# More Strassen pairs in the gate and up projections of a decoder layer, with the residual stored in DRAM meanwhile and some lo parts formed by a DMA

## Chip, cores and metric

The kernel runs on one core of a Trainium2 chip. The metric is the device time of one execution in microseconds; the median of three runs of the kernel before is 1488.6 us (1488.46 to 1488.66). All data are float32 and 256 tokens are processed.

## The reference

One decoder layer on 256 tokens of width 2048: a mixer (state space heads beside gated short convolutions), a cross-attention to 256 memory tokens, and a SwiGLU feed-forward network of width 5632, each behind an RMSNorm and added to the residual, with a last RMSNorm. What the change touches is the feed-forward network:

```
def swiglu(h, w_gate, w_up, w_down):
    return (jax.nn.silu(h @ w_gate) * (h @ w_up)) @ w_down

h = h + swiglu(rmsnorm(h, norm_ffn[i]), w_gate[i], w_up[i], w_down[i])
```

## The kernel before

**Products in three passes.** TensorE multiplies float32 rounded to a shorter form (fp32r). Each operand is therefore kept as a sum hi + lo of two such numbers, and a product is hi*hi + lo*hi + hi*lo, three matmuls.

**The weight stream.** All weights lie in DRAM in the order of use, as chunks of 128 partitions x 1024 numbers (512 KB): two blocks of 128 rows of a weight matrix by 512 columns. `load_to` (L197) issues their loads on SyncE's queue (SP), each into one of six raw buffers, as soon as one is free. `split_to` makes hi and lo of a chunk: ScalarE copies the raw chunk into h with rounding (L236), VectorE subtracts, l = raw - h (L237). There are four h and four l buffers, so a chunk's copy waits until TensorE has read the h of the chunk four back.

**Plain chunks.** `tok_mm` multiplies one chunk with the two blocks of 128 tokens: first eight matmuls with h (L310, L311), then four with l (L314), twelve in all.

**Blocks of the feed-forward network.** Gate (g) and up (u) are made in 11 blocks (n = 0 to 10) of 512 columns. For each, eight chunks of g and eight of u (c = 0 to 7) are summed in four PSUM accumulators, (g, u) x (two token blocks). `ffn_units` gives the order of the chunks, also that of the weight stream; a unit is one chunk, two, or a pair.

**Strassen pairs.** In blocks 1 to 8 (`SEVEN`) the chunks c = 0 and 1 of g and u are taken as pairs: chunk c of g with chunk c of u, a 2 x 2 product of blocks, in seven products in place of eight (Winograd's form). With three passes that is 21 matmuls for the pair (`seven_mm`, L982 to L985), where two plain chunks have 24. A pair needs sums of weight blocks: `pair_sums` makes four half-chunk sums on VectorE (L211 to L214) and hi and lo of three of them (copies on ScalarE, L218; subtractions on VectorE, L219), six slots of 128 x 512. It needs sums of token blocks, made once by `token_sums` and kept. And four of the seven products go to four shared PSUM accumulators, from which `p_post` forms corrections (one copy on ScalarE, L936; four operations on VectorE, L937 to L940) once the block's last pair is done. `whole` adds a correction to each of the four accumulators of g and u when they are evacuated (L1207).

**After a block.** `g_post` and `u_post` form silu(g) * u (L1216, L1224), turn it by 32 x 32 transposes on VectorE (L329), write it to DRAM (`put`, L342) and read it back transposed (`get`, L349), both on SP, and keep hi and lo of it (L1234, L1235) in four slots for the down projection.

**Slots.** One pool of 63 slots of 128 x 512 holds, in the feed-forward network: the residual (`res`, 8), the normed input (`h2g`, 16), the gated products (4 a block, in the end 44), and the parts of pairs (6 each). The residual is next used when the down projection's pairs and sums are added to it (`p_post`, `d_evac`).

**Order of work.** TensorE and SP run in the order of the code. On ScalarE, VectorE and GpSimd a planner of the framework orders the instructions at build time, by its estimate of when each is ready, with those earlier in the code going first. Work behind a block is written as generators: `step`, called once in each unit after its first part, moves each one to its next `yield`. `ahead_of(i, f)` calls f just ahead of the load of chunk i on SP's queue.

Of the kernel before, what the change touches and what calls it, by code (L numbers as in the profile page):

```python
# [17 lines left out]
F32 = mybir.dt.float32  # L18
F32R = mybir.dt.float32r
AF = mybir.ActivationFunctionType  # L20
ALU = mybir.AluOpType
# [3 lines left out]
T = 256  # L25
# [2 lines left out]
FF = 5632  # L28
FT = FF // 128
FN = FF // 512  # L30
SEVEN = range(1, 9)
OUT_GAPS = (2, 5, 4, 5)
GAPS = (2, 4, 5, 4, 5, 4)
H = 32
# [38 lines left out]
def ffn_units():  # L73


    o = [[((m, 0, c),)] for h in range(2) for m in "gu" for c in range(4 * h, 4 * h + 4)]
    for n in range(1, FN):
        if n in SEVEN:
            for q, rest in ((0, "g2 g3 g4 u2 u3 u4"), (1, "g5 g6 g7 u5 u6 u7")):
                o.append([(("g", n, q), ("u", n, q))])  # L80
                k = [(a[0], n, int(a[1])) for a in rest.split()]
                o += [[(a,), (b,)] for a, b in zip(k[0::2], k[1::2])]
        else:
            o += [[((m, n, c),), ((m, n, c + 1),)] for m in "gu" for c in range(0, KT // 2, 2)]
    return o
# [34 lines left out]
def stream_plan():  # L120

    p = [(("a0",), 512), (("b0",), 512)]
    p += [(("ab", kt), 1024) for kt in range(1, KT)]
    for n in range(2, 22):
        p += [(("in", n, c), 1024) for c in range(KT // 2)]
    p += [(("wo", n, c), 1024) for n, c in out_order()]
    p += [(k, 1024) for k in order_of(out_units())]
    p += [((m, c), 1024) for m in "kqv" for c in range(KT // 2)]
    p += [(("o", n, c), 1024) for n in range(4) for c in range(2)]
    p += [(k, 1024) for k in order_of(ffn_units() + down_units())]  # L130
    return p


def trunk(tc, wst, vecs, xp, xtp, mp, mtp, wdt_in, nfin, outp):
    nc = tc.nc
    plan = stream_plan()
    index = {k: i for i, (k, _) in enumerate(plan)}
    offs, o = [], 0
# [5 lines left out]
    with ExitStack() as ctx:  # L144
# [12 lines left out]
        drp = E(tc.tile_pool(name="scr", bufs=1, space=DRAM))  # L157
# [5 lines left out]
        def nm(s):  # L163
            cnt[0] += 1
            return f"{s}{cnt[0]}"

        def slot(shape=(128, 512), dt=F32):
            return sp.tile(list(shape), dt, tag="s", name=nm("s"))
# [11 lines left out]
        act = nc.scalar.activation  # L180
        tt = nc.vector.tensor_tensor
# [23 lines left out]
        def pair_sums(key, u):  # L205


            g = held.pop(key)
            a, b = slice(0, 512), slice(512, 1024)
            f = bp.tile([128, 1024], F32, tag="b", name=nm("b"))  # L210
            tt(f[:, a], g[:, a], u[:, a], ALU.add)  # L211
            tt(u[:, a], u[:, a], u[:, b], ALU.add)  # L212
            tt(f[:, b], f[:, a], u[:, b], ALU.add)
            tt(g[:, a], f[:, b], g[:, b], ALU.add)  # L214
            pair_parts[key] = []
            for x in (f[:, a], f[:, b], g[:, a]):
                h, l = slot(dt=F32R), slot(dt=F32R)
                nc.scalar.copy(h, x)  # L218
                tt(l, x, h.bitcast(F32), ALU.subtract)  # L219
                pair_parts[key].append((h, l))  # L220

        def split_to(n):
            while nsplit[0] < min(n, len(plan)):
                i = nsplit[0]
                key, w = plan[i]
                r = raws.pop(i)
                if key in first_of:
                    held[key] = r
                elif key in second_of:
                    pair_sums(second_of[key], r)  # L230
                h = hip.tile([128, 1024], F32R, tag="h", name=nm("h"))
                l = lop.tile([128, 1024], F32R, tag="l", name=nm("l"))
                m = 2 if i in (0, 2) else 1
                for j in range(m):
                    c = slice(j * w // m, (j + 1) * w // m)
                    nc.scalar.copy(h[:, c], r[:, c])  # L236
                    tt(l[:, c], r[:, c], h[:, c].bitcast(F32), ALU.subtract)  # L237
                los[i] = l
                his[i] = h
                nsplit[0] += 1  # L240
# [28 lines left out]
        def small(name):  # L269
            return cp.tile([128, 2], F32, tag=name, name=nm(name), bufs=4)  # L270
# [84 lines left out]
        procs = []  # L355
# [68 lines left out]
        def ahead_of(i, f):  # L424
            before.setdefault(i, []).append(f)
# [437 lines left out]
        res = [[None] * 4 for _ in range(2)]  # L863
# [27 lines left out]
        def wait(k):  # L891
            for _ in range(k):
                yield
# [24 lines left out]
        def token_scale(name, sums, factor=None):  # L918

            e = small("rv")  # L920
            with tc.high_priority():
                nc.vector.tensor_reduce(e, sums, axis=mybir.AxisListType.X, op=ALU.add)
            r = inv_rms(e, D)
            out = cp.tile([128, 2], F32, name=name)
            ts(out, r, 1.0 if factor is None else factor, None, ALU.mult)
            return out


        shared, seven_a = {}, {}
# [19 lines left out]
            return  # L949
            yield  # L950

        def token_sums(key, parts):


            xy = fp.tile([128, 1024], F32, tag="f", name=nm("f"))
            w = 512 // len(parts)
            for i, (hi, lo) in enumerate(parts):
                tt(xy[:, i * w:i * w + w], hi.bitcast(F32), lo.bitcast(F32), ALU.add)
            a11, a21, a12, a22, *o = [xy[:, i * 128:i * 128 + 128] for i in range(8)]
            tt(o[0], a21, a22, ALU.subtract)  # L960
            tt(o[1], a11, o[0], ALU.subtract)
            tt(o[2], a21, a11, ALU.subtract)
            tt(o[3], a12, o[1], ALU.subtract)
            seven_a[key] = []
            for i in range(2):
                h, l = [tp.tile([128, T], F32R, tag="t", name=nm("t")) for _ in range(2)]
                y = xy[:, 512 + i * T:512 + i * T + T]
                nc.scalar.copy(h, y)
                tt(l, y, h.bitcast(F32), ALU.subtract)
                seven_a[key] += [(h[:, j * 128:j * 128 + 128], l[:, j * 128:j * 128 + 128]) for j in range(2)]  # L970
# [71 lines left out]
        for i, parts in enumerate(units_o):  # L1042
            for j in (i, i + 1, i + 2):
                if j < len(units_o) and len(units_o[j][0]) == 2 and units_o[j][0][0] not in seven_a:
                    c = units_o[j][0][0][2]
# [6 lines left out]
            _, n, c = keys[0]  # L1052
# [90 lines left out]
        h2g = {}  # L1143
        h2s = cp.tile([128, 2, 4], F32, name="h2s")
        ff = {}

        def o_post(n, accs):
            add_to_res(n, accs, h2s)
            if n == 3:
                ff["r"] = token_scale("fscale", h2s)  # L1150
            if n == 0:
                yield
            yield from to_features(n, "nffn", h2g, None if n == 0 else (4, 1, 0) if n == 1 else (6, 2, 1))
# [23 lines left out]
        with tc.high_priority():  # L1177
            for mb in range(2):
                Vs.append(slot())
                c = scales["mem"][:, mb:mb + 1]  # L1180
# [21 lines left out]
        def whole(m, n, tb, ps):  # L1202

            if n not in SEVEN:
                return ps
# [34 lines left out]
        def part_mm(part):  # L1240
            m, n, c = part[0]
            if len(part) == 2:
                g, u, p = faccs["g", n], faccs["u", n], shared[n]
                seven_mm(part, side_blocks(h2g, 2 * c), seven_a[c], g, u, p,
                         p + [g[0], g[1], u[0]] if c == 0 else [], p if c == 1 else [])
                return
            start = c == 0
            if n in SEVEN:
                start = (1,) if (m, c) == ("u", 2) else False
            tok_mm(faccs[m, n], part[0], side_blocks(h2g, 2 * c), (0, 1), start, c == KT // 2 - 1)  # L1250

        for i, parts in enumerate(ffn_units()):
            if i == len(ffn_units()) - 3:
                token_sums(("d", 0, 0), [gs[0]])
            if i == 8:
                for c in range(2):
                    token_sums(c, [(h2g[2 * c + k][:, 0:T], h2g[2 * c + k][:, T:]) for k in range(2)])
            post = []
            for part in parts:
                m, n, c = part[0]  # L1260
                for k in part:
                    if k[2] == 0:
                        faccs[k[:2]] = [acc(), acc()]
                if len(part) == 2:
                    if c == 0:
                        shared[n] = [msc() for _ in range(4)]
                    else:
                        post.append(p_post(n, shared[n]))
                elif c == KT // 2 - 1:
                    post.append((g_post if m == "g" else u_post)(n, faccs[m, n]))  # L1270
            unit([(list(part), lambda part=part: part_mm(part)) for part in parts], post or None)
# [123 lines left out]
        for i, parts in enumerate(units):  # L1395
# [7 lines left out]
            if len(parts[0]) == 2:  # L1403
                _, n, c = keys[0]
# [4 lines left out]
            n = keys[-1][1]  # L1409
# [136 lines left out]
```

## Time and profile before

| | |
|---|---|
| Median of three runs | 1488.6 us (1488.46 to 1488.66) |
| Profiled execution | span 1487.0 us, first to last instruction; the runs' median is 1.6 us above it |
| TensorE clock granted | 0.998 |
| TensorE matmul, VectorE, ScalarE busy | 99%, 77%, 56% of the span |
| GpSimd busy | 2% |
| DMA | 346.71 MB, mean 233 GB/s |

In the pages and tables that follow, PE is TensorE's matmuls, PEld its weight loads, DVE VectorE, ACT ScalarE, POOL GpSimd, SP SyncE. A row of a group gives line, engine, operation, what it writes and reads, the count, busy time and mean duration, and then how long the engine was idle just before and for whom it waited. A row in order of time gives start and duration in us. Line numbers are those of the kernel before.

Of the span, block 1 of the feed-forward network begins at 822.7 us, block 9 at 1160.0, block 10 at 1203.5, and the down projection at 1247.0.

### The profile page before, as it was taken

What the parts mean: (1) busy time and instruction counts of PE and PEld (TensorE: products, weight loads), DVE (VectorE), ACT (ScalarE), POOL (GpSimd) and SP (SyncE); (2) the same over time, 40 slices, a digit from 0 to 9 for tenths busy, and PEclk for the clock granted to TensorE, in tenths of its full rate; (3) what the DMA queues carried; (4) which work ended last, traced back from release to release, by engine and by line L of the source; (5) the groups of instructions that cost most, each with busy time, mean ns of one, the idle gap of its engine ahead of it and who ended that gap; (6) DMA issues with size and microseconds to landing.
All of it is one profiled execution on the core that took longest, in us unless ns stands there. A gap on an engine that the chain in (4) does not pass through costs nothing.

```text
span 1487.0 us, 18685 instructions
## 1 busy us (share of the span) xinstructions
PE 1476.3 (99%) x6637; PEld 1216.9 (82%) x6637; DVE 1138.9 (77%) x1596; ACT 837.1 (56%) x1176; POOL 33.8 (2%) x46
## 2 busy tenths in 40 slices
PE   9999999999999999999999999999999999999997
PEld 7788888888888888888888888888888888888886
DVE  6677777776785775997577888888887667979975
ACT  7576654867654554665465555555554444655553
POOL 0001000101000000000000000000000000000000
PEclk9999999999999999999999999999999999999999
DMA  9886766868767675768747676665667665765553
GB/s 361 275 282 227 268 225 219 289 225 308 235 214 278 212 233 198 267 228 283 265 159 237 234 248 212 231 213 206 232 226 245 223 225 198 240 215 196 201 189 108
DMA packets 149214, 346.71 MB, mean 233 GB/s; under 512 B 11360, under 2 KB 62976, under 8 KB 149120
## 3 DMA queue, kind: packets, MB, share of 16 engines
q1 hardware_dynamic: 140064, 338.64, 65.6%
q10 hardware_dynamic: 9056, 6.87, 1.5%
q8 instruction: 52, 0.85, 0.2%
q14 instruction: 42, 0.34, 0.1%
HBM read 321.30 MB, written 24.17 MB: 232 GB/s over the span
## 4 chain that ended last, share of the span: by engine, by line
PE 98%; DMA 0%; issue 0%; SPq 0%; ACT 0%; DVE 0%; DVEq 0%; POOLq 0%; POOL 0%
PE a L310 28%; PE a L311 28%; PE a L314 28%; PE m L985 2%; PE m L983 2%; PE m L982 2%; PE a L982 1%; PE a L985 1%; PE a L983 1%; PE m L731 1%; PE m L314 0%; PE m L310 0%; PE m L311 0%; DMA r<-in_w_dram 0%; PE m L1139 0%
## 5 line engine op out<-in xcount | busy, mean ns | idle before, releaser
L237 DVE TENSOR_TENSOR l<-r,h 128x1024 fp32r<-128x1024 f32 (+1 forms) x539 | 650.7, 1215 | 231.3 <-ACT h L236 220.3
L236 ACT CAST h<-r 128x1024 fp32r<-128x1024 f32 (+1 forms) x539 | 562.2, 1047 | 468.4 <-PE a L311 310.2
L310 PE MATMUL a<-h,s 128*128 128x512 f32 x1855 | 726.3, 392 | 0.4 <-ACT h L236 0.4
L311 PE MATMUL a<-h,s 128*128 128x512 f32 x1855 | 722.5, 389 | 0.0
L314 PE MATMUL a<-l,s 128*128 128x512 f32 x1855 | 498.9, 389 | 0.0
L310 PEld LDWEIGHTS a<-h,s 128*128 128x128 f32 x1855 | 348.5, 188 | 74.7 <-issue 2.0
L314 PEld LDWEIGHTS a<-l,s 128*128 128x128 f32 x1855 | 348.4, 188 | 72.5
L311 PEld LDWEIGHTS a<-h,s 128*128 128x128 f32 x1855 | 348.6, 188 | 71.5
L218 ACT CAST s<-b 128x512 fp32r<-128x512 f32 x64 | 38.7, 616 | 23.5 <-DVE b L211 19.8
L329 DVE STREAM_TRANSPOSE b<-s 128x512 f32<-128x512 f32 x62 | 40.7, 689 | 6.4 <-ACT s L336 6.4
L219 DVE TENSOR_TENSOR s<-b,s 128x512 fp32r<-128x512 f32 x64 | 43.2, 683 | 0.0
L672 DVE SCALAR_TENSOR_TENSOR t<-t,vec,t 128x255 f32<-128x255 f32 (+2 forms) x72 | 33.1, 490 | 3.9 <-ACT t L669 3.2
L211 DVE TENSOR_TENSOR b<-r,r 128x512 f32<-128x512 f32 x32 | 21.9, 685 | 14.3 <-DMA r<-in_w_dram 14.2
L336 ACT ACTIVATE s<-a,xr 128x512 f32<-128x512 f32 x42 | 26.4, 679 | 3.6 <-PE a L314 3.6
L1207 DVE TENSOR_TENSOR f<-a,f 128x512 f32<-128x512 f32 x32 | 20.5, 683 | 8.5 <-PE a L314 8.4
L985 PE MATMUL m<-s,t 128*128 128x512 f32 x64 | 24.9, 389 | 0.0
L982 PE MATMUL m<-s,t 128*128 128x512 f32 x64 | 24.9, 389 | 0.0
L983 PE MATMUL m<-s,t 128*128 128x512 f32 x64 | 24.9, 389 | 0.0
L218 ACT CAST s<-r 128x512 fp32r<-128x512 f32 x32 | 19.8, 617 | 6.0 <-DVE r L214 5.9
L212 DVE TENSOR_TENSOR r<-r 128x512 f32<-128x512 f32 x32 | 22.0, 686 | 0.4
L1234 ACT CAST s<-f 128x512 fp32r<-128x512 f32 x22 | 13.5, 619 | 15.4 <-DMA f<-w 15.4
L219 DVE TENSOR_TENSOR s<-r,s 128x512 fp32r<-128x512 f32 x32 | 21.8, 683 | 0.4 <-ACT s L218 0.4
(232 smaller groups left out, 1058.2 us busy)
## 6 DMA issues: line engine op xcount, KB each, us to landing
r<-in_w_dram SPq DMA_DIRECT2D x535, 512.0 KB, 4.6
w<-b SPq DMA_DIRECT2D x42, 512.0 KB, 3.3
f<-w SPq DMA_DIRECT2D x42, 512.0 KB, 4.9
s<-acsT ACTq DMA_DIRECT2D x24, 256.0 KB, 5.3
s<-in_xt_dram SPq DMA_DIRECT2D x16, 256.0 KB, 6.6
s<-in_mt_dram SPq DMA_DIRECT2D x8, 256.0 KB, 6.1
s<-in_m_dram SPq DMA_DIRECT2D x8, 256.0 KB, 5.9
s<-in_x_dram SPq DMA_DIRECT2D x7, 256.0 KB, 7.4
```

What stands on the lines that cost most here:

```text
L218: nc.scalar.copy(h, x)
L219: tt(l, x, h.bitcast(F32), ALU.subtract)
L236: nc.scalar.copy(h[:, c], r[:, c])
L237: tt(l[:, c], r[:, c], h[:, c].bitcast(F32), ALU.subtract)
L310: mm(ps[tb], ah, h[:, w], start=first and i == ks[0], stop=False)
L311: mm(ps[tb], al, h[:, w], start=False, stop=False)
L314: mm(ps[tb], blocks(i, tb)[0], l[:, i * 512:i * 512 + 512], start=False, stop=stop and i == ks[-1])
L329: nc.vector.transpose(t[:, tb * 512:tb * 512 + 512], src[tb])
L672: stt(a[:, d:], u[:, 0:T - d], v("cw", 4 * ct + k), a[:, d:], ALU.mult, ALU.add)
L982: mm(ps, ah, bh, start=any(ps is q for q in start), stop=False)
L983: mm(ps, al, bh, start=False, stop=False)
L985: mm(ps, ah, bl, start=False, stop=any(ps is q for q in stop))
```

## The change

- `SEVEN` now says how many pairs a block has: three in blocks 1 to 9, two in block 10. With three pairs the order of a block's chunks is: pair 0, g3, g4, u3, pair 1, g5, u4, g6, pair 2, g7, u5, u6, u7 (before: pair 0, g2, g3, g4, u2, u3, u4, pair 1, g5, g6, g7, u5, u6, u7, which block 10 now has).
- `token_sums` is also called for c = 2; its hi and lo go to two slots, which are kept through the blocks.
- In blocks 1 to 10 the lo part of the chunks g4 and g6 (`BY_DMA`) is no longer made by VectorE. ScalarE copies the raw chunk into h and writes l = -h; then a DMA issued by GpSimd adds the raw chunk to l.
- Twelve units after each `o_post`, the residual's two tiles of its 512 columns are written to DRAM on SP (`park`); their slots are then free. Ahead of the loads of the down projection's chunks ("d", 0, 10) to ("d", 0, 17), one tile each, they are read back into new slots (`unpark`).

```diff
-SEVEN = range(1, 9)
+SEVEN = {n: 3 if n < 10 else 2 for n in range(1, 11)}
+BY_DMA = {(m, n, c) for n in range(1, 11) for m, c in (("g", 4), ("g", 6))}
...
-            for q, rest in ((0, "g2 g3 g4 u2 u3 u4"), (1, "g5 g6 g7 u5 u6 u7")):
+            plan = {2: ("g2 g3 g4 u2 u3 u4", "g5 g6 g7 u5 u6 u7"),
+                    3: ("g3 g4 u3", "g5 u4 g6", "g7 u5 u6 u7")}[SEVEN[n]]
+            for q, rest in enumerate(plan):
                 o.append([(("g", n, q), ("u", n, q))])
                 k = [(a[0], n, int(a[1])) for a in rest.split()]
-                o += [[(a,), (b,)] for a, b in zip(k[0::2], k[1::2])]
+                o += [[(a,) for a in k[i:i + 2]] for i in range(0, len(k), 2)]
...
-                m = 2 if i in (0, 2) else 1
+                if key in BY_DMA:
+                    nc.scalar.copy(h, r)
+                    act(l, h.bitcast(F32), AF.Identity, scale=-1.0)
+                    nc.gpsimd.dma_start(l.bitcast(F32), r, accum_op=ALU.add)
+                m = 0 if key in BY_DMA else 2 if i in (0, 2) else 1
...
-        def token_sums(key, parts):
+        def token_sums(key, parts, wide=False):
...
+            if wide:
+                h, l = slot(dt=F32R), slot(dt=F32R)
+                nc.scalar.copy(h, xy[:, 512:])
+                tt(l, xy[:, 512:], h.bitcast(F32), ALU.subtract)
+                seven_a[key] = [(h[:, j * 128:j * 128 + 128], l[:, j * 128:j * 128 + 128]) for j in range(4)]
+                return
...
+        parked = drp.tile([2, 4, 128, 512], F32, name="parked")
+
+        def park(n):
+
+            yield from wait(12)
+            for tb in range(2):
+                nc.sync.dma_start(parked[tb, n], res[tb][n])
+                yield
+
+        def unpark(tb, n):
+            res[tb][n] = slot()
+            nc.sync.dma_start(res[tb][n], parked[tb, n])
+
+        for n in range(4):
+            for tb in range(2):
+                ahead_of(index[("d", 0, 10 + 2 * n + tb)], lambda tb=tb, n=n: unpark(tb, n))
+
         def o_post(n, accs):
             add_to_res(n, accs, h2s)
             if n == 3:
                 ff["r"] = token_scale("fscale", h2s)
+            procs.append(park(n))
...
-                         p + [g[0], g[1], u[0]] if c == 0 else [], p if c == 1 else [])
+                         p + [g[0], g[1], u[0]] if c == 0 else [], p if c == SEVEN[n] - 1 else [])
...
-                start = (1,) if (m, c) == ("u", 2) else False
+                start = (1,) if (m, c) == ("u", SEVEN[n]) else False
...
-                for c in range(2):
-                    token_sums(c, [(h2g[2 * c + k][:, 0:T], h2g[2 * c + k][:, T:]) for k in range(2)])
+                for c in range(3):
+                    token_sums(c, [(h2g[2 * c + k][:, 0:T], h2g[2 * c + k][:, T:]) for k in range(2)], c == 2)
...
-                    else:
+                    elif c == SEVEN[n] - 1:
                         post.append(p_post(n, shared[n]))
```

## The prediction

> **What bounds the kernel now.** I read the page first, then the busy time by stage, then the order of time around a pair of blocks.
>
> ```profile
> span 1487.0 us, 18685 instructions
> PE 1476.3 (99%) x6637; PEld 1216.9 (82%) x6637; DVE 1138.9 (77%) x1596; ACT 837.1 (56%) x1176; POOL 33.8 (2%) x46
> q1 hardware_dynamic: 140064, 338.64, 65.6%
> PE 98%; DMA 0%; issue 0%; SPq 0%; ACT 0%; DVE 0%; DVEq 0%; POOLq 0%; POOL 0%
> L310 PE MATMUL a<-h,s 128*128 128x512 f32 x1855 | 726.3, 392 | 0.4 <-ACT h L236 0.4
> r<-in_w_dram SPq DMA_DIRECT2D x535, 512.0 KB, 4.6
> w<-b SPq DMA_DIRECT2D x42, 512.0 KB, 3.3
> ```
>
> The chain of waits is TensorE at 98%, and in the whole span its largest group waited 0.4 us. So time can be gained only by matmuls that are not issued, and anything that is late costs its full delay. Nothing else in the change can win time.
>
> ```profile
> 777.00:822.70 45.70, 45.70 (x203) 37.86 (x202) 35.35 (x59) 27.67 (x43) 0.80 (x1) 1.00 0.70 231
> 1033.50:1075.70 42.20, 42.20 (x188) 34.94 (x187) 36.03 (x45) 22.80 (x28) 0.00 (x0) 1.00 0.64 226
> 1160.00:1203.50 43.50, 43.50 (x193) 36.05 (x192) 24.39 (x25) 19.11 (x21) 0.00 (x0) 1.00 0.63 218
> 1203.50:1247.00 43.50, 43.50 (x193) 36.05 (x192) 27.31 (x36) 19.61 (x24) 0.00 (x0) 1.00 0.67 230
> 1247.00:1260.00 13.00, 13.00 (x58) 10.69 (x58) 12.95 (x17) 7.27 (x9) 0.00 (x0) 1.00 0.44 147
> 1260.00:1270.00 10.00, 10.00 (x46) 8.27 (x45) 10.00 (x15) 6.32 (x9) 0.00 (x0) 1.00 0.98 333
> ```
>
> The columns are the stretch and its length, then busy time of PE, PEld, DVE, ACT and POOL (each with its instructions), granted clock, DMA share and GB/s. The rows are the end of block 0, a block with two pairs (one of blocks 1 to 8), blocks 9 and 10 (no pairs), and the start of the down projection. PE is full in each. DVE is the engine to watch: 36.03 of 42.20 us in a block with pairs, and all of it just after 1247.
>
> **The gain: 39 matmuls.** A pair replaces two chunks of 12 matmuls by 21 products, so it saves 3. Blocks 1 to 8 get one more pair each, block 9 gets three, block 10 two: 8 + 3 + 2 = 13 pairs, 39 matmuls. The price of one, in order of time:
>
> ```profile
> 990.23 0.39 PE L311 MATMUL a<-h,s 128*128 128x512 f32 x1
> 991.36 0.39 PE L982 MATMUL m<-h,s 128*128 128x512 f32 x1
> 992.04 0.39 PE L983 MATMUL a<-h,s 128*128 128x512 f32 x1
> 1009.72 0.39 PE L310 MATMUL a<-h,s 128*128 128x512 f32 x1
> 1012.44 0.39 PE L982 MATMUL m<-h,s 128*128 128x512 f32 x1
> 1017.20 0.39 PE L310 MATMUL a<-h,s 128*128 128x512 f32 x1
> ```
>
> A plain chunk takes 1009.72 to 1012.44, 2.72 us for 12, a pair 1012.44 to 1017.20, 4.76 us for 21: 0.227 us each. So 39 x 0.227 = **8.8 us** go. As a cross-check, the block without pairs takes 43.5 and the block with two takes 42.2, 0.65 a pair, 8.4 for 13.
>
> **DVE in the blocks.** Its instructions overlap a little, so I take start to start:
>
> ```profile
> 991.33 1.29 DVE L1207 TENSOR_TENSOR f<-a,f 128x512 f32<-128x512 f32 x2 [1.05 <-PE a L314]
> 992.54 1.41 DVE L1224 SCALAR_TENSOR_TENSOR g<-f,fscale,g 128x512 f32<-128x512 f32 x2
> 993.86 1.30 DVE L329 STREAM_TRANSPOSE b<-g 128x512 f32<-128x512 f32 x2
> 995.08 3.46 DVE L237 TENSOR_TENSOR l<-r,h 128x1024 fp32r<-128x1024 f32 x3
> 1008.60 1.29 DVE L219 TENSOR_TENSOR s<-b,s 128x512 fp32r<-128x512 f32 x2
> ```
>
> Three splits in 3.46 make (3.46 - 1.22) / 2 = 1.12 each, two halves in 1.29 make 0.60. A third pair adds seven half-width operations (L211 to L219), 7 x 0.60 = 4.2; two lo parts taken by DMA remove 2 x 1.12 = 2.2. DVE goes from 36.0 to 38.0 while the block shrinks to 183 x 0.227 = 41.5: 92%. Block 9 is 24.39 + 3 x 4.2 + 8 x 0.60 (the four corrections of L937 to L940 and the four of L1207) - 2.2 = 39.6 at most; its window already holds two of these L1207, so 38.4. The tightest place is the second pair, which now starts 21 + 36 matmuls, 12.9 us, after the block (before: 21.1). DVE has there the gate evacuation 991.33 to 995.16 (3.8), a split of the chunk u3, the pair's own 4.2 and two splits: 3.8 + 4.2 + 3 x 1.12 = 11.4 of 12.9, and the pair's last sums are not read before about 3 us into it. It fits, and the chunk behind g3, whose split now waits behind the evacuation until 995.08, is just the one that the DMA takes. I cost it at 0; if DVE's order leaves it idle, rival B has the price. The new third set of token sums is seven operations of at most 0.60, 4.2 at most, in block 0, where DVE has 10 us free.
>
> **ACT.** Two negations and three half casts more a block:
>
> ```profile
> 990.70 1.05 ACT L236 CAST h<-r 128x1024 fp32r<-128x1024 f32 x1 [1.67 <-PE a L311]
> 992.51 1.05 ACT L236 CAST h<-r 128x1024 fp32r<-128x1024 f32 x1 [0.76 <-PE a L983]
> 1007.29 1.14 ACT L218 CAST s<-b 128x512 fp32r<-128x512 f32 x2
> 1254.04 2.00 ACT L236 CAST h<-r 128x1024 fp32r<-128x1024 f32 x2
> ```
>
> 2 x 0.95 + 3 x 0.52 = 3.5 on 22.80 of 41.5. Cost 0: 63% busy.
>
> **The adding DMA** is the unknown term: no run shows one, nor any DMA issued by POOL. First its window. A cast starts 0.47 us after the last hi matmul of the chunk four back (990.23 to 990.70; 992.04 to 992.51), cast and negation take 2.00. For g4 the chunk four back is the last of the block before: its last hi matmul lies 1.13 before the block (990.23, 991.36), so l is ready for the add at -1.13 + 0.47 + 2.00 = +1.34. PE reads l after the pair, g3 and eight matmuls of g4: 41 x 0.227 = 9.3. The window is **7.9 us**. For g6 it is the g of the second pair, whose last hi matmul comes 0.68 in: +3.15, read after 21 + 12 + 12 + 8 = 53 matmuls, 12.0: **8.9 us**. In block 10 the two change places; so ten DMAs with 7.9 and ten with 8.9.
>
> Then its length; a DMA's issue I take from a put's:
>
> ```profile
> 1249.66 0.38 SPq L342 DMA_DIRECT2D w<-b  x1
> ```
>
> 338.64 MB took 65.6% of 1487 us, so 512 KB take 1.5 us of all 16 engines, and the put's 3.3 us are 1.8 fixed and 1.5 of data. At least, the add is a put: 3.3. At most it reads two operands and lands like two weight loads one behind the other, 2 x 4.6 = 9.2. I take 1.8 + 2 x 1.5 for two operands + 1.5 for one load beside it (DMA is busy 0.64) + 0.4 to issue = 6.7, nearer to the upper end. That is inside both windows: cost **0**, with 1.2 us to spare. At 9.2 it costs 10 x 1.3 + 10 x 0.3 = 16. The raw buffer is held until the add lands, 1.34 + 6.7 = 8.0 after the block's start; the second of the three splits of 995.08 freed it at 997.4, 6.0 after. The load six places on, g6, then lands at 8.0 + 4.6 = 12.6, ahead of its cast at 12.9 + 0.68 + 0.47 = 14.1: cost 0, with 1.5 to spare.
>
> A rule of the Trainium skill speaks against this DMA (SBUF — State Buffer, § Who interferes with whom): GpSimd writes such a DMA's descriptors through a port pair which a DVE instruction in a two-port mode locks. By the same section a tensor_tensor has no such mode. The trace can only show that the split, 1.22 us for 1024 elements against 0.68 for 512, runs at one steady rate. By the rule the sum stays as it is.
>
> **Queues.** SP issues 8 parking stores and 8 reloads of 256 KB, 0.4 us each, and 16 x 0.75 = 12 us of data, half in block 0 (DMA share 0.70), half at the start of the down projection, where the share reaches 0.98 and transfers already land late (1247 to 1300):
>
> ```profile
> f<-w SPq DMA_DIRECT2D x1, 512.0 KB, 6.8
> s<-in_nfin_dram SPq DMA_DIRECT2D x2, 256.0 KB, 8.7
> ```
>
> Behind a reload on SP stand weight loads. They run up to six chunks ahead, 6 x 2.72 = 16.3 us; less a landing of 8.7 and cast and split of 2.2, 5.4 are left, and five reloads in a row make a load 3.8 late. I take 0, bounds 0 and 2. POOL has nothing else queued behind its DMAs, and of a parking store the waiting is long over when it is issued.
>
> **The start of the down projection** has no slack. Block 10 now ends with two more L1207:
>
> ```profile
> 1247.01 1.41 DVE L1224 SCALAR_TENSOR_TENSOR g<-a,fscale,g 128x512 f32<-128x512 f32 x2 [1.09 <-PE a L314]
> 1253.31 1.22 DVE L237 TENSOR_TENSOR l<-r,h 128x1024 fp32r<-128x1024 f32 x1
> 1254.75 0.40 PE L985 MATMUL m<-l,t 128*128 128x512 f32 x1
> ```
>
> DVE starts the evacuation at 1247.01 and works without a gap to the split 1253.31 to 1254.53; PE reads that l at 1254.75, 0.2 later. 2 x 0.60 = 1.2 ahead of it in the same order stalls PE by **1.0**. Bounds 0 (another order) and 1.2.
>
> **The sum.** 1487.0 - 8.8 + 1.0 = 1479.2 of span. The runs' median of 1488.6 is 1.6 above this execution's span, so 1480.8. Own range of this case 1479.4 to 1483.
>
> **Rivals.**
> A, the slower one: the adding DMA lands after PE wants l. From 7.9 us on ten of them stall PE, from 8.9 all twenty; 10 x (L - 7.9) eats the remaining 7.8 at L = 8.7. Behind the waiting matmul stands all of PE. At 9.2 the time is 1480.8 + 16 = 1497. For it: two operands, weight loads at 0.64 beside it, landings of 6.8 and 8.7 in a crowd. Against: 6.7 as worked out.
> B, DVE becomes the bound. In the block its waits for others were 42.2 - 36.0 = 6.2 us; 3.5 are left. If all of them stay, 2.7 a block are lost, 10 x 2.7 = 27: 1508. Most are early arrivals, which shrink when DVE is fuller:
>
> ```profile
> L237 DVE TENSOR_TENSOR l<-r,h 128x1024 fp32r<-128x1024 f32 x16 | 19.3, 1216 | 2.3 <-ACT h L236 2.3
> L1207 DVE TENSOR_TENSOR f<-a,f 128x512 f32<-128x512 f32 x5 | 3.3, 684 | 2.1 <-PE a L314 2.1
> ```
>
> If it loses anything, then some 0.5 us a block: 5 in all, 1486.
> C, POOL cannot issue while DVE runs: from 991.33 to 998.54 DVE has no gap, so g4's add starts at +7.2 and lands at 13.9 against 9.3; ten times 4.6 are 46: 1527. No row speaks for or against it, since POOL does nothing in these blocks.
> The page named above would have C for two-port modes alone, which these are not.
> D, the pairs of blocks 9 and 10 do not pay: parking frees 8 of 63 slots, and by my count in block 9 are 36 for the gated products, 16 for the normed input, 2 for the third sums and 6 for a pair's parts, 60. If parts wait for slots, the five pairs' 3.4 us come back: 1484.2.
>
> **How the numbers follow.** The forecast has 0.54, A 0.24, B 0.12, D 0.06, C 0.04. A run tells a difference from none at about 0.2%, 3 us. Faster: all 0.54, 0.06 of A, 0.05 of B, 0.05 of D: 0.70. Same: 0.03 + 0.03 + 0.01: 0.07. Slower: 0.15 + 0.04 + C: 0.23. Below 1479.4 lies little, since the full 8.8 without any stall is 1479.8. Up to 1492 A is in to L of about 9.0, and most of B; 0.15 stays above.
>
> **What would show it.** PE at 6598 matmuls (or so many fewer as records lack), blocks of 41.5 us; the adding DMA landing in under 7.9 us and no wait of L314 or L985 on it; DVE at 38 us a block; a PE gap of about 1 us near the first pair of the down projection. PE waits of L314 on a DMA in every block say A, waits of L982 to L985 on DVE say B, and a landing right at the end of DVE's unbroken stretches says C.

## The result, and the profile after

The kernel after the change takes 1502.1 us (median; 1500.5 to 1503.8), the kernel before 1488.6 beside it (1488.5 to 1488.8): a ratio of 1.0092 [1.0077, 1.0106]. It is **slower by 13.5 us**, where 1480.8 was forecast, and it lies above the range. The profiled execution, the slowest of the four, took 1503.8 us with a span of 1502.1.

The page of the kernel after: span, engines, the queue of GpSimd's DMAs, the shares of the chain of waits, two groups and three DMA issues.

```profile
span 1502.1 us, 18868 instructions
PE 1477.5 (98%) x6598; PEld 1209.6 (81%) x6598; DVE 1178.0 (78%) x1690; ACT 875.6 (58%) x1238; POOL 53.9 (4%) x66
q0 software_dynamic: 2880, 10.49, 3.6%
PE 82%; DVE 8%; DMA 6%; issue 2%; ACT 1%; SPq 0%; DVEq 0%; POOLq 0%; POOL 0%; ACTq 0%
L321 PE MATMUL a<-l,s 128*128 128x512 f32 x1751 | 473.1, 390 | 8.3 <-DMA l<-r 8.1
L239 POOL DMA_DIRECT2D l<-r x20 | 17.5, 873 | 436.5 <-ACT l L238 243.2
l<-r POOLq DMA_DIRECT2D x20, 512.0 KB, 5.8
parked<-s SPq DMA_DIRECT2D x8, 256.0 KB, 8.4
s<-parked SPq DMA_DIRECT2D x8, 256.0 KB, 7.8
```

The 39 matmuls are gone (6637 to 6598), and yet the chain is no longer TensorE alone: DVE has 8% of it and DMA 6%. The matmuls with lo parts (L321, before L314) now wait for `l<-r`, the adding DMA. That DMA itself lands a median 5.8 us after its issue, and the issue comes some 0.4 behind the negated h: 6.2 in all, which is not longer than the forecast's 6.7. In what follows L200 (before L197) is the weight load on SP, L214 the first sum of a pair's parts, L237 to L239 copy, negation and adding DMA of a `BY_DMA` chunk, L243 and L244 copy and split of any other, L349 and L356 put and get, L995 to L998 the pair's matmuls, L1237 the correction at the evacuation, L1264 ScalarE's copies of the product that the get reads back.

Next the busy time from block 2 to the end of block 10, in the kernel after and then in the same kernel without the adding DMA (the first experiment). In parentheses is what was issued; in x4 below, where TensorE never waits in this stretch, it is 1691 matmuls.

```profile
867.00:1250.00 383.00, 370.14 (x1600) 298.56 (x1599) 329.10 (x436) 227.24 (x280) 15.54 (x18) 1.00 0.73 243
```

```profile
867.00:1250.00 383.00, 382.12 (x1686) 316.18 (x1685) 364.15 (x472) 221.09 (x274) 0.00 (x0) 1.00 0.64 229
1033.00:1075.00 42.00, 42.00 (x187) 34.76 (x187) 40.39 (x53) 24.21 (x30) 0.00 (x0) 1.00 0.63 226
```

The kernel after gets 86 matmuls less through in the same time, 86 x 0.227 = 19.5 us of the 23.2 by which the two spans differ (1502.1 and 1478.9). Of the rest, 1.4 us lie ahead of block 1, which begins at 823.9 in place of 822.5 (not followed further), and 1.1 in a slow stretch just behind 1250 (in the last section). For whom TensorE waited there (the weight loads' waits: total, times, longest):

```profile
PEld a L321 <- DMA l<-r: 12.9, 12, 4.2
PEld a L995 <- DVE f L1237: 7.6, 9, 1.1
PEld m L998 <- DVE l L244: 2.2, 4, 1.0
```

So there are two kinds of stall: the adding DMA lands too late, and VectorE evacuates the accumulators too late.

### The profile page after: what moved, and what is told of

It is laid out like the page before. It is cut to its first block, busy times and chain, and to the rows that moved or that the text cites. A ratio compares the mean times of both kernels' runs of the same rounds, so it can differ in the third digit from the quotient of the medians.

```text
span 1502.1 us, 18868 instructions
## 1 busy us (share of the span) xinstructions
PE 1477.5 (98%) x6598; PEld 1209.6 (81%) x6598; DVE 1178.0 (78%) x1690; ACT 875.6 (58%) x1238; POOL 53.9 (4%) x66
## 4 chain that ended last, share of the span: by engine, by line
PE 82%; DVE 8%; DMA 6%; issue 2%; ACT 1%; SPq 0%; DVEq 0%; POOLq 0%; POOL 0%; ACTq 0%
PE a L321 23%; PE a L317 23%; PE a L318 23%; DMA r<-in_w_dram 3%; DVE l L244 3%; DMA l<-r 2%; PE m L998 2%; PE m L996 2%; PE m L995 2%; PE a L995 1%; PE a L998 1%; PE a L996 1%; DVE s L222 1%; DVE f L1237 1%; ACT h L243 1%
## 5 line engine op out<-in xcount | busy, mean ns | idle before, releaser
L244 DVE TENSOR_TENSOR l<-r,h 128x1024 fp32r<-128x1024 f32 (+1 forms) x519 | 627.3, 1216 | 190.8 <-ACT h L243 175.9
L243 ACT CAST h<-r 128x1024 fp32r<-128x1024 f32 (+1 forms) x519 | 539.6, 1045 | 334.0 <-PE a L318 223.9
L317 PE MATMUL a<-h,s 128*128 128x512 f32 x1751 | 686.7, 392 | 0.6 <-ACT h L243 0.6
L318 PE MATMUL a<-h,s 128*128 128x512 f32 x1751 | 683.1, 390 | 0.0
L321 PE MATMUL a<-l,s 128*128 128x512 f32 x1751 | 473.1, 390 | 8.3 <-DMA l<-r 8.1
L321 PEld LDWEIGHTS a<-l,s 128*128 128x128 f32 x1751 | 328.3, 188 | 80.8 <-DMA l<-r 12.9
L317 PEld LDWEIGHTS a<-h,s 128*128 128x128 f32 x1751 | 329.4, 188 | 71.0 <-issue 1.8
L318 PEld LDWEIGHTS a<-h,s 128*128 128x128 f32 x1751 | 329.6, 188 | 67.7
L214 DVE TENSOR_TENSOR b<-r,r 128x512 f32<-128x512 f32 x45 | 30.8, 685 | 50.4 <-DMA r<-in_w_dram 49.0
L222 DVE TENSOR_TENSOR s<-b,s 128x512 fp32r<-128x512 f32 x90 | 61.5, 683 | 0.1
L239 POOL DMA_DIRECT2D l<-r x20 | 17.5, 873 | 436.5 <-ACT l L238 243.2
L217 DVE TENSOR_TENSOR r<-b,r 128x512 f32<-128x512 f32 x45 | 30.7, 683 | 0.2
L216 DVE TENSOR_TENSOR b<-b,r 128x512 f32<-128x512 f32 x45 | 30.7, 683 | 0.0
L1237 DVE TENSOR_TENSOR f<-a,f 128x512 f32<-128x512 f32 x40 | 26.3, 679 | 2.8 <-PE a L321 2.8
```

Source lines behind the costliest of these rows:

```text
L317: mm(ps[tb], ah, h[:, w], start=first and i == ks[0], stop=False)
L318: mm(ps[tb], al, h[:, w], start=False, stop=False)
L321: mm(ps[tb], blocks(i, tb)[0], l[:, i * 512:i * 512 + 512], start=False, stop=stop and i == ks[-1])
L1237: tt(c, ps, c, op)
```

## The experiments

None of these kernels leaves out a part of the computation. Beside each, the kernel before ran on the same chip (medians 1488.45, 1488.61 and 1488.41 in the three groups). The loss to be explained is 1502.1 - 1480.9 = 21.2 us against the first experiment.

| kernel | us | ratio to before | matmuls in 867 to 1250 |
|---|---|---|---|
| after | 1502.1 | 1.0092 [1.0077, 1.0106] | 1600 |
| x1, no adding DMA | 1480.9 | 0.9949 [0.9936, 0.9961] | 1686 |
| x2, before with the adding DMA | 1510.7 | 1.0158 [1.0141, 1.0176] | 1608 |
| x3, before with parking | 1488.4 | 1.0000 [0.9991, 1.0009] | 1692 |
| x4, two pairs a block, no adding DMA | 1486.9 | 0.9990 [0.9982, 0.9999] | 1691 |
| z1, a seventh raw buffer | 1507.0 | 1.0122 [1.0108, 1.0136] | 1587 |
| y2, adding DMA for g4 alone | 1481.2 | 0.9957 [0.9944, 0.9969] | 1685 |
| y3, adding DMA for g6 alone | 1501.9 | 1.0091 [1.0077, 1.0105] | 1602 |
| y4, x1 with the down projection's first pair later | 1479.7 | 0.9939 [0.9925, 0.9952] | 1692 |
| w1, own raw buffer for g4 and g6 | 1486.0 | 0.9985 [0.9976, 0.9994] | 1673 |
| w2, get one unit later | 1493.6 | 1.0043 [1.0028, 1.0059] | 1640 |
| w4, x1 with an adding DMA that nobody reads | 1486.2 | 0.9985 [0.9977, 0.9994] | 1669 |
| w5, w1 and w2 | 1480.9 | 0.9950 [0.9936, 0.9964] | 1686 |

The theories at the start. Theory 1: the adding DMA holds its raw buffer longer than a split does, SP stands in order behind that buffer, and the loads of the next pair come late. Theory 2: VectorE is too full with three pairs (rival B). Theory 3: the adding DMA is late by its own length (rival A). Theory 4 came with the later runs: the negated h of g6 is itself late, because g6's raw load stands on SP behind the put and the get.

Four results lie outside every range that was given for them: x2 (1494 at most), z1 (1481 to 1488 or 1497 to 1503), w2 (1481 to 1489 or 1495 to 1503) and w4 (1480 to 1483 or 1488 to 1500).

### Which part loses the time: x1 to x4

x1 takes the adding DMA away and leaves all lo parts to VectorE:

```diff
-BY_DMA = {(m, n, c) for n in range(1, 11) for m, c in (("g", 4), ("g", 6))}
+BY_DMA = set()
```

> The change with all lo parts made by VectorE again; three pairs and parking stay. Theory 1 (the adding DMA keeps its raw buffer, SP stands behind it for 65.6 us in blocks 2 to 10, the next pair's loads come late, VectorE first idles on them for 38 us and is then behind): without it the 23 us of stalls shrink to under 12, so under 1491. Theory 2 (VectorE is simply too full: 92% with the DMA, and 2 x 1.12 us more a block without it, 40.2 of 41.5): the stalls grow by up to 10 x 2.2 = 22, so 1505 to 1524. Whether SP's waits on l vanish and VectorE's waits on raw loads shrink tells the two apart in the trace.

x2 puts the adding DMA alone into the kernel before:

```diff
+BY_DMA = {(m, n, c) for n in range(1, 11) for m, c in (("g", 4), ("g", 6))}
...
-                m = 2 if i in (0, 2) else 1
+                if key in BY_DMA:
+                    nc.scalar.copy(h, r)
+                    act(l, h.bitcast(F32), AF.Identity, scale=-1.0)
+                    nc.gpsimd.dma_start(l.bitcast(F32), r, accum_op=ALU.add)
+                m = 0 if key in BY_DMA else 2 if i in (0, 2) else 1
```

> The kernel before with the lo parts of g4 and g6 of blocks 1 to 10 by the adding DMA, and nothing else of the change. Theory 1: in the old order a pair is loaded every 21 us, so a raw buffer held 6 to 7 us longer is felt less; loads still come some us later, stalls of 0 to 5, 1488.6 to 1494. Theory 2: VectorE has less to do, no stall, 1488.6. Theory 3 (the adding DMA is late by its own length, 5.0 to 7.8 us from l = -h to its landing): ten windows of 7.9 and more hold it, so 1488.6 to 1490.

x3 puts `park` and `unpark` alone into the kernel before (the lines of these two functions and of their calls in the diff of the change, nothing else):

```diff
+            for tb in range(2):
+                nc.sync.dma_start(parked[tb, n], res[tb][n])
+                yield
...
+            res[tb][n] = slot()
+            nc.sync.dma_start(res[tb][n], parked[tb, n])
...
+            procs.append(park(n))
```

> The kernel before with the residual parked in DRAM and read back, and nothing else. All theories: 16 transfers of 256 KB under a stream of weights that is ahead, 1488.6 plus 0 to 2 at the start of the down projection.

x4 has neither the third pair nor the adding DMA, but pairs in blocks 9 and 10 and parking:

```diff
-SEVEN = {n: 3 if n < 10 else 2 for n in range(1, 11)}
-BY_DMA = {(m, n, c) for n in range(1, 11) for m, c in (("g", 4), ("g", 6))}
+SEVEN = {n: 2 for n in range(1, 11)}
+BY_DMA = set()
...
-                for c in range(3):
+                for c in range(2):
```

> Two pairs in each of blocks 1 to 10 (two blocks more than before), the residual parked, no adding DMA, no third token sums. Twelve matmuls less than before, 12 x 0.227 = 2.7 us. All theories expect the blocks without stalls; the start of the down projection costs 1.0 to 1.5 as in the change, so 1486.9 to 1487.4. If the two new blocks stall for slots, 1488.6 or above.

x1 comes to 1480.9, so the whole loss goes with the adding DMA. VectorE then works 40.39 of 42.00 us in a block with three pairs (the second row of x1 above), 96%, and TensorE does not wait once: **theory 2 falls**, and with it what the adding DMA was to relieve. The only wait of TensorE's matmuls left in x1 from 867 to 1250, in order of time:

```profile
1246.70 0.50 PE L998 MATMUL m<-l,t 128*128 128x512 f32 x1 [0.88 <-DVE l L244]
```

The matmul before it started at 1245.43, so this one is 1.27 behind instead of 0.227, and the next follows after 0.34: 1.15 us, the stall forecast for the start of the down projection. x3 shows no difference, with an interval of 1.3 us to either side, so parking by itself costs no more than that. x4 saves four pairs, 12 x 0.227 = 2.7, less that stall: 1.6 expected from the rows, 1.5 measured (by its interval 0.1 to 2.7). Pairs in blocks 9 and 10 pay as expected, as far as that can be told.

x2 loses 22.3 us, which none of the theories had expected, in an order of work where VectorE has room (271.09 of 383 us busy in the same stretch). Its waits, SP's and then TensorE's, and the DMA's time to landing:

```profile
SPq L198 <- DMA l<-r: 90.6, 20, 8.0
...
PEld a L319 <- DMA l<-r: 21.5, 13, 3.2
...
DMA to landing us min/median/max: 7.5/8.7/10.2
```

Here all of TensorE's waits are for the adding DMA, which takes 8.7 instead of 5.8. So in this kernel theory 3 has its share; but SP stands behind the DMA's buffer too, 20 times.

### Which of the two DMAs, and how: z1, y2, y3

z1 gives a seventh raw buffer (and two slots less):

```diff
-        rawp = E(tc.tile_pool(name="raw", bufs=6))
+        rawp = E(tc.tile_pool(name="raw", bufs=7))
...
-        sp = E(tc.tile_pool(name="slots", bufs=63))
+        sp = E(tc.tile_pool(name="slots", bufs=61))
```

> The change with seven raw buffers in place of six, paid for with two of the 63 slots (61). Theory 1 (the adding DMA keeps its raw buffer, the loads behind it on SP come late, VectorE and ScalarE fall behind, and only through that the next l = -h and its DMA are late too): SP's waits on l vanish, VectorE's 38 us of waits on raw loads shrink, the stalls fall from 23 to under 8, so 1481 to 1488. Theory 3 (the adding DMA lands late by itself, by its length and by the transfers beside it, whatever the loads do): 1497 to 1503.

y2 and y3 keep one of the two:

```diff
+BY_DMA = {("g", n, 4) for n in range(1, 11)}
```

> The change with the adding DMA for g4 alone; g6 goes back to VectorE. Theory 1: in the change SP waits behind g6's DMA just ahead of u7 and the next block's first pair, so with g4 alone the loads of that pair are in time; ten DMAs of 5 to 6.5 us in windows of 7.9: 1481 to 1485. Theory 3: about half of the change's loss, 1489 to 1493.

```diff
+BY_DMA = {("g", n, 6) for n in range(1, 11)}
```

> The change with the adding DMA for g6 alone; g4 goes back to VectorE. Theory 1: most of the loss stays, 1493 to 1502. Theory 3: about half of it, 1489 to 1493.

It is **g6's DMA alone**: y3 keeps the whole loss, y2 has none in the median (two of its five executions took 1484). y2 also gains nothing over x1 (1481.2 to 1480.9), although it spares VectorE ten splits. SP's waits from 820 to 1250, of y2 and of y3:

```profile
SPq L200 <- DVE l L244: 252.7, 98, 6.6
```

```profile
SPq L200 <- DVE l L244: 205.8, 73, 6.4
SPq L200 <- DMA l<-r: 74.1, 10, 7.8
```

In y2 no weight load waits for the adding DMA; in y3 one does in each of ten blocks, 7.4 us on average. The seventh buffer does not change it: in z1 SP still stands 77.0 us behind the DMA, nine times, and the kernel is slower still, 1507.0; why it is slower stays open. A load waits for one buffer that the order of the program gives it, not for whichever is free, so one more only changes which load it is; that reading is inferred from z1, and w1 below, with as many buffers and slots, speaks for it.

### The way from g6's buffer to the stalls

One round of it, at the start of block 5 in the kernel after. First SP's waits from 970 to 980, then VectorE, ScalarE (the negation of g4; the wait for the get, the copy and the negation of g6), GpSimd, TensorE (the first matmul of pair 0, a wait in it, the first of pair 1) and SP in order of time:

```profile
SPq L200 <- DMA l<-r: 7.5, 1, 7.5
```

```profile
984.95 0.69 DVE L214 TENSOR_TENSOR b<-r,r 128x512 f32<-128x512 f32 x1 [3.63 <-DMA r<-in_w_dram]
...
998.43 1.28 DVE L1237 TENSOR_TENSOR f<-a,f 128x512 f32<-128x512 f32 x2
```

```profile
997.64 1.06 ACT L238 ACTIVATE l<-h 128x1024 fp32r<-128x1024 f32 x1
...
1011.95 0.62 ACT L1264 CAST s<-f 128x512 fp32r<-128x512 f32 x1 [2.83 <-DMA f<-w]
...
1013.94 1.04 ACT L237 CAST h<-r 128x1024 fp32r<-128x1024 f32 x1
1015.02 1.06 ACT L238 ACTIVATE l<-h 128x1024 fp32r<-128x1024 f32 x1
```

```profile
999.11 0.85 POOL L239 DMA_DIRECT2D l<-r  x1 [26.34 <-DVE f L1237]
1016.49 0.86 POOL L239 DMA_DIRECT2D l<-r  x1 [16.53 <-DVE b L214]
```

```profile
994.73 0.39 PE L995 MATMUL m<-h,s 128*128 128x512 f32 x1
...
999.17 0.50 PE L995 MATMUL a<-h,t 128*128 128x512 f32 x1 [0.64 <-DVE f L1237]
...
1008.64 0.39 PE L995 MATMUL m<-h,s 128*128 128x512 f32 x1
```

```profile
1002.28 0.38 SPq L349 DMA_DIRECT2D w<-b  x1
...
1005.44 0.38 SPq L356 DMA_DIRECT2D f<-w  x1
1005.92 18.03 SPq L200 DMA_DIRECT2D r<-in_w_dram  x10
```

The same places of SP in x1, whose block 5 starts at 988.39, where that of the kernel after starts at 994.73:

```profile
992.82 0.38 SPq L349 DMA_DIRECT2D w<-b  x1
...
995.83 0.38 SPq L356 DMA_DIRECT2D f<-w  x1
996.30 10.39 SPq L200 DMA_DIRECT2D r<-in_w_dram  x7
```

1. The adding DMA of block 4's g6 still reads its raw buffer; SP waits 7.5 us for it. Behind that load on SP stand those of the next block's first pair.
2. VectorE, which needs them for the pair's sums, stands still for 3.63 us up to 984.95. From then on it works without a gap but is behind: the evacuation with corrections (L1237) begins 3.7 us after the block's start, in x1 0.6 after (988.97). TensorE waits for it (999.17).
3. With the evacuation the put is late, 7.55 us after the block's start (x1: 4.43), and the get behind it, 10.71 (x1: 7.44). The load of g6 is the next on SP: 11.2 (x1: 7.9). It lands at 1013.2, 18.4 after the block's start; in x1 12.9.
4. ScalarE does not take it up at once. It has stood 2.83 us for the get's landing (1011.92), and the copies that come before g6's in its order keep it until 1013.94, 0.78 behind the landing of g6's raw chunk. So the negated h of g6 is ready at 1016.08 and the DMA issued at 1016.49, and TensorE wants l 53 matmuls behind pair 1's first, 1008.64 + 53 x 0.227 = 1020.7: 4.6 us are left where 8.9 were forecast. For g4 it is ready at 998.70 and wanted at 1005.01: 6.3 where 7.9 were forecast, since ScalarE's own order is late too.
5. The adding DMA lands late, and holds the buffer later still, from which step 1 starts again for block 6. From one block's start to the next, the kernel after takes 41.5 us in block 1, then 41.9, 44.7, 42.8, 43.9, 44.8, 43.2, 42.6 and 42.3 in block 9, where x1 takes 41.5 in each. The first block loses nothing, and from the third on the loss stays between 0.8 and 3.3 a block.

VectorE's waits for a weight load ahead of a pair's sums tell the same of all blocks, 867 to 1250, in the kernel after and in x1:

```profile
DVE b L214 <- DMA r<-in_w_dram: 40.2, 13, 5.1
```

```profile
DVE b L214 <- DMA r<-in_w_dram: 0.9, 3, 0.4
```

### Opening the loop: w1, w2, w4, w5

w1 takes the holding away: the chunks g4 and g6 get a raw buffer of their own, so nobody else waits for it.

```diff
+        ownp = E(tc.tile_pool(name="own", bufs=1))
...
-        sp = E(tc.tile_pool(name="slots", bufs=63))
+        sp = E(tc.tile_pool(name="slots", bufs=61))
...
-                r = rawp.tile([128, 1024], F32, tag="r", name=nm("r"))
+                r = (ownp if plan[i][0] in BY_DMA else rawp).tile([128, 1024], F32, tag="r", name=nm("r"))
```

> The change with a raw buffer of their own for g4 and g6 of each block (one for both in turn; 61 slots), so that no other weight load on SP is ever given the buffer that an adding DMA still reads. Theory 1 (SP standing behind g6's raw buffer makes the next pair late, and with it all that follows): the loss goes, 1481 to 1486. Theory 3 (the adding DMA of g6 is late by its own 7 to 10 us, whatever SP does): 1496 to 1503.

w2 issues the get one unit later, so that g6's load goes ahead of it. ScalarE's copies of what the get reads move too:

```diff
             w = put(t)
             yield
+            yield
             d = get(w)
```

> The change with the read-back of the gated product put one unit later on SP, so that g6's raw load stands ahead of it. Theory 4 (g6's l = -h starts late because its raw load stands behind put and get: it landed 18.5 us after the block's start, against 12.9 where nothing stalls): about 3 us more room for g6's DMA, the stalls fall from 23 to under 10, 1481 to 1489. Theory 1 and theory 3: little changes, 1495 to 1503.

w4 is x1 (all lo parts by VectorE) with an adding DMA of g6's raw chunk into a tile that nobody reads, and 61 slots: holding, without a reader.

```diff
+SHADOW = {("g", n, 6) for n in range(1, 11)}
...
-        sp = E(tc.tile_pool(name="slots", bufs=63))
+        sp = E(tc.tile_pool(name="slots", bufs=61))
...
+                if key in SHADOW:
+                    nc.gpsimd.dma_start(shadow, r, accum_op=ALU.add)
```

> Three pairs and parking with all lo parts by VectorE (1480.9), and beside them an adding DMA of each block's raw g6 into a tile that nothing reads (61 slots). TensorE waits for no adding DMA here; it only takes DMA time and keeps its raw buffer. Theory 1: the buffer alone is enough, SP stands behind it and the next pair is late, 1488 to 1500. Theory 3: without TensorE's wait nothing is lost, 1480 to 1483.

w5 is w1 and w2 together:

```diff
...
+                r = (ownp if plan[i][0] in BY_DMA else rawp).tile([128, 1024], F32, tag="r", name=nm("r"))
...
             w = put(t)
             yield
+            yield
             d = get(w)
```

> A raw buffer of their own for g4 and g6 and the read-back one unit later, both. Theory 1 or 4: no loss left, 1480 to 1484. Theory 3: 1493 to 1503.

SP's waits in w4 and TensorE's (L1242 is there the evacuation's correction):

```profile
SPq L201 <- DMA shadow<-r: 57.5, 10, 7.2
...
PEld a L1000 <- DVE f L1242: 4.7, 5, 1.1
```

w4 loses 5.3 us against x1 though TensorE never needs the DMA's result: **holding the buffer alone costs**, by late evacuations. It is not the added transfers or the two slots: w5 has twenty such DMAs and 61 slots and loses nothing. The holding as w4 has it (57.5 us of SP's waits, where the kernel after has 72.8) makes a quarter of the 21.2; the rest came only in kernels in which TensorE reads the DMA's result. w1 brings 16.1 of the 21.2 back, with the memory that z1 has: what counts is whose load stands behind the DMA. What remains in w1 is g6's DMA late by itself, for which TensorE waits 5.0 us. w2 brings 8.5, while SP stands 89.4 us behind the buffers. With both, w5, the loss is gone: 1480.9, like x1 to 0.1. The parts are not to be added (16.1 and 8.5 exceed 21.2), as they are cuts into one loop.

w2 does not work as theory 4 has it. ScalarE's waits for the get and for g6's raw chunk, 867 to 1250, in the kernel after:

```profile
ACT s L1264 <- DMA f<-w: 18.2, 9, 5.1
...
ACT h L237 <- DMA r<-in_w_dram: 0.4, 1, 0.4
```

The table has means over blocks 2 to 9, from the traces; the first three columns are times after the block's start, the room is from the negated h to where TensorE wants l (53 matmuls behind pair 1's first, as in step 4), and the last column is the median of g6's DMA alone, from issue to landing.

| kernel | g6's raw chunk lands | its copy starts | l = -h ready | room | DMA of g6 |
|---|---|---|---|---|---|
| after | 17.5 | 18.1 | 20.2 | 5.9 | 5.8 |
| w2 | 14.1 | 18.0 | 20.6 | 5.2 | 4.8 |
| w1 | 13.9 | 14.6 | 16.8 | 8.2 | 7.5 |
| w5 | 11.6 | 15.5 | 18.1 | 6.9 | 5.2 |

The later get lets the raw chunk land earlier, but g6's copy gains nothing by it: in w2 ScalarE stands for the get, which is later itself, and starts the copy 0.5 us after the get's landing, 3.3 to 5.2 after that of the raw chunk. The room does not grow; it shrinks by 0.7 and, from w1 to w5, by 1.3. What becomes shorter is the adding DMA, by 1.0 and by 2.3. SP's waits for the put's landing, ahead of the get, in w1 and in w5; then the two kernels while block 5's DMA of g6 is under way (the column before the last is the DMA share):

```profile
SPq L357 <- DMA w<-b: 28.7, 10, 5.2
```

```profile
SPq L357 <- DMA w<-b: 9.2, 10, 1.4
```

```profile
1006.60:1014.40 7.80, 7.80 (x37) 6.43 (x36) 7.22 (x10) 4.82 (x6) 0.84 (x1) 1.00 0.97 310
```

```profile
1006.60:1012.30 5.70, 5.70 (x27) 4.73 (x26) 5.68 (x9) 4.25 (x6) 0.86 (x1) 1.00 0.78 201
```

In w1 four or five weight loads are under way when g6's DMA is issued, and it takes 6.7 to 8.2 us; in w5 three or four, and it takes 5.1 to 6.6 (blocks 2 to 9). So **theory 1 holds**, for the larger part. **Theory 3 holds for the rest**, but with a length that the transfers beside it make, not one of the DMA's own. **Theory 4 falls in w2's trace**, though w5 came to the time that it gave. That the later get shortens the DMA by spreading the loads is argued from these rows; no run tests it alone. Whether w5's two edits also mend x2, where the DMA takes 8.7, was not tried.

### A version that beats both: y4

y4 is x1 with the first pair of the down projection one plain chunk later and the last norm's gain loads two chunks later:

```diff
-GAPS = (2, 4, 5, 4, 5, 4)
+GAPS = (3, 4, 5, 4, 5, 3)
...
-            before.setdefault(index[("d", 0, 9 + 2 * n)], []).append(lambda n=n: load_gain(n))
+            before.setdefault(index[("d", 0, 11 + 2 * n)], []).append(lambda n=n: load_gain(n))
```

> Three pairs and parking without the adding DMA (1480.9), and in the down projection three plain chunks instead of two ahead of its first pair (three instead of four ahead of the last), the loads of the final gain two chunks later. The one stall left, 1.2 us at the first pair of the down projection, where VectorE runs without a gap, gets 2.7 us of room: 1479.5 to 1480.1. If the tail pays instead: 1481 to 1482.

The stall at the start of the down projection is gone. The busy time of that stretch, in x1 and in y4:

```profile
1235.00:1260.00 25.00, 24.12 (x107) 19.64 (x106) 23.26 (x32) 12.59 (x17) 0.00 (x0) 1.00 0.68 235
```

```profile
1235.00:1260.00 25.00, 25.00 (x112) 20.69 (x111) 23.02 (x37) 12.37 (x17) 0.00 (x0) 1.00 0.67 239
```

Five matmuls more in 25 us are the 1.1 us. y4 takes 1479.7 us, 0.9939 [0.9925, 0.9952] of before: all pairs, no adding DMA, the lowest time here, though its interval overlaps that of x1.

## Why the prediction was wrong, step by step

- **The gain of 39 matmuls, 8.8 us: right.** The count is 6598, and x1, which still has the stall of 1.15, gains 7.5 where 8.8 - 1.15 = 7.65 were to be expected.
- **The stall at the start of the down projection, 1.0: right**, 1.15 in x1, from the cause named (two corrections more ahead of the split).
- **DVE in the blocks, 38.0 of 41.5, cost 0: right in cost.** With all splits on VectorE it was 40.39 of 42.00 and still cost nothing. Rival B's losses did not come. Its sign did: matmuls of the pairs (now L995 to L998) waited for DVE, 10.3 us from 867 to 1250. But VectorE was late there because the loads were; in x1, where it has more to do, one such wait of 1.3 us is left, at the start of the down projection. The wrong conclusion was in the change's premise, which the forecast took over: two lo parts by DMA relieved an engine that did not need it.
- **The adding DMA's length, 6.7: right enough for this kernel**, 5.8 in the median from issue to landing and 6.2 from the negated h. The upper bound of 9.2 was passed by little, 9.5 to landing. But it is not one length: for g6 it was 4.8 in w2 and 7.5 in w1.
- **Its windows, 7.9 and 8.9: wrong.** They were 6.3 and 4.6 in block 5. They were worked out from the hi matmuls of the chunk four back, as though ScalarE's copy waited for nothing but its buffer. For g6 the raw chunk landed 5.5 us later after the block's start than in x1, and ScalarE had the copies of the read-back to make before.
- **"The load six places on, g6, then lands at 8.0 + 4.6 = 12.6, ahead of its cast at 12.9 + 0.68 + 0.47 = 14.1: cost 0, with 1.5 to spare": the step that failed.** The load landed at 18.4. In x1 it lands at 12.9 with the cast at 14.1, but that the first is near 12.6 is chance: no DMA holds a buffer there, and the load stands behind the get, issued at 7.4. So two things were left out. The load stands behind the put and the get on SP, so it moves with the evacuation. And the step was done for g4's buffer alone: what stands behind **g6's** buffer, the loads of the next block's first pair, which VectorE waits for, was not asked. That term was 0 in the sum; with the holding gone, 16.1 of the 21.2 us come back (w1), and the rest with a shorter DMA as well (w5).
- **Queues.** Parking 0: right within x3's interval, though a reload took 7.8 and a parking store 8.4 us; how five reloads would make a load 3.8 late is not worked out there. "POOL has nothing else queued" was true and beside the point: the queue that mattered was SP's, behind the buffer.
- **Rival A** had the right place, a wait of L321 on `l<-r`, and 1497 at L = 9.2. It had the wrong condition: it made the length decide, from 8.7 up, while the time went at 5.8, by windows that shrank. In w1, where the room is 8.2, near the forecast, and g6's DMA takes 7.5, A's stall is what remains. It also had no price for the late evacuations, 7.6 of the waits. **Rival C** fell: GpSimd issues g4's DMA of block 5 at 999.11 for 0.85 us while VectorE works without a gap from 984.95 to 1011.0, and it is read unhindered at 1005.01. **Rival D** fell with x4 and with x1, where block 9 has three pairs and TensorE waits for none.
- **The range** reached to A at a length of 9.0 and so to 1492. That a late transfer makes the next block's later was in none of the terms, so their bounds did not cover it. The lower end of 1479.4 is 0.4 below what the terms give, 1479.8; nothing hung on it.

## What to carry to other kernels

A transfer that reads a buffer of a ring holds it until it lands: ask, for each such buffer, which load is next in line for it, what stands behind that load in an in-order queue, and who waits for those, before costing the transfer at nothing. Compute a window from all that its start waits for (the load of the raw data and its place in the queue too, not only the buffer), and check whether its end feeds back into the next round's start; then the bounds of single terms do not bound the cost. Take the length of a transfer as what the transfers beside it make of it: the same 512 KB took 4.6 to 9.5 us in one kernel here. And take work off an engine only where the bound engine waits for it: at 96% busy, VectorE cost nothing here.

## What the runs showed of the hardware

**The clock after a stall.** In the kernel after TensorE stood idle for 3.79 us (to 1247.47); then seven matmuls came at 0.43 us each instead of 0.227. By stretch, in the kernel after and in x2 (the eighth column is the granted clock):

```profile
1243.00:1248.00 5.00, 1.21 (x6) 0.70 (x5) 2.64 (x6) 1.45 (x2) 0.00 (x0) 1.00 0.82 222
1248.00:1252.00 4.00, 4.00 (x12) 3.12 (x12) 2.19 (x4) 0.41 (x1) 0.00 (x0) 0.58 0.87 311
```

```profile
900.00:904.00 4.00, 4.00 (x11) 3.17 (x12) 3.69 (x5) 0.62 (x1) 0.00 (x0) 0.58 0.72 269
991.00:995.00 4.00, 4.00 (x19) 3.31 (x18) 3.70 (x6) 1.92 (x3) 0.00 (x0) 1.00 0.78 255
```

The granted clock was 0.58 for those 4 us, which costs 7 x 0.2 = 1.4 us on top of the stall. In x2 an idle time of 2.47 us (to 899.91) was followed by it and one of 2.77 (to 990.60) was not, so the length of the stall alone does not decide. The Trainium skill (TensorE: Matmul & The Clock Gate, § Part 1: The HAM clock gate) has the clock halve after an idle window of about 3.4 us that runs free of the program. The slow matmuls agree with a half clock, and the free phase with its coming after one stall and not the other; that an idle time of 2.47 us was enough does not agree with a whole window of 3.4.

**The adding DMA's price.** 3.6% of 16 engines' 1502.1 us for 20 DMAs are 2.7 us of all engines each, against 1.5 for a weight load of the same 512 KB. GpSimd is busy 0.87 us with an issue, where 0.4 had been taken from a put.
